# One run of products per group, dt in four column tiles, and two scalings moved to VectorE in a Mamba-2 and attention trunk

## The chip, the cores and the metric

The kernel runs on one core of a Trainium2 chip. The metric is the device time of one execution in microseconds (us). Five engines take part: TensorE (PE in the profile, its weight loads PEld), VectorE (DVE), ScalarE (ACT), GpSimd (POOL) and SyncE (SP, which only issues DMAs here). Each engine works through its own list of instructions in order and waits on semaphores for the others.

## The reference

Two layers on a 512 x 1024 input: a Mamba-2 mixer with a chunked state-space scan, then differential attention, then a final norm. The change lies in the first layer, of which this is the core (cut):

```python
h = rms_norm(x, norm_g)
zxbcdt = h @ w_in                                   # z, xBC, and dt_raw (32 heads)
xbc = silu(causal_depthwise_conv(xbc, conv_w, conv_b))
dt = softplus(dt_raw + dt_bias)
a = -exp(a_log)
# per chunk:
acs = cumsum(a * dt);  decay = exp(where(causal, acs_l - acs_s, -inf))
y_diag = (C_l . B_s) * decay  @  (x * dt)           # products inside the chunk
y_off  = C_l . state * exp(acs)
y = y_diag + y_off + d_skip * x
y = group_rms_norm(y * silu(z)) * gate_norm_g       # 8 groups of 4 heads
x = x + y @ w_out
```

## The kernel before

All of the first layer is kept on the chip. Sequence positions are cut into four chunks of 128 (`NQ`), the 32 heads into eight groups of four (`G`, `R`). Large products are split in a high and a low float32r part and run as three matmuls of 128x128 by 512 (`mm3`); small products of the scan are plain float32, which the profile shows as two records each.

TensorE's dense stream in the first layer is `z0 g0 g1 z1 g2 g3 z2 g4 o0 g5 z3 g6 g7 o1 o2 o3`: `z` are gate projections (tile `pz`), `g` the B, C and x projections of one group (tile `pg`), `o` the output projections (tile `po`). Each needs four banks of PSUM from a pool of four (`mm_bank`). A `pg` bank comes free when VectorE has run the convolution on it: one multiplication (`pg<-pg,ar_row`), a pass on ScalarE, and three `xc` steps with 511, 510 and 509 columns, of which the last frees the bank. Weights arrive by DMA in tile `raw`; ScalarE makes the high part `whi`, VectorE the low part `wlo`.

Beside the stream runs `ssd(g)`, the scan of a group. `pcb` is C.B; `pxt` turns x, and VectorE makes `xdt` (x times dt) and `dx` (x times the skip factor) from it; GpSimd makes `xe` for the states; `psA` and `psB` are the chunk states, `pyd` the products inside the chunks (64 columns of weights each, so two lie side by side in the array), `po1` and `po2` (both shown as `po<-hst,xc`) the parts from earlier chunks. Then `dx` is summed, gated with `zs`, its squares summed on ScalarE (`tmp,ss<-dx`), `rsqrt` makes the factor in a chain of small VectorE instructions (`v`, `y_i`, `y_y`, `y_c`, last `y_y`), ScalarE scales the four chunks (`tmp<-dx,y_y`), `pyt` turns them, and `yh`, `yl` are the high and low part for the output projection.

`dt` is made once, near the start, and all groups need it. Its chain is: product `ps_dt`, tile `pre` (times `ar_row`, the 1/rms of each position along a row, which comes from the product `aps_r`), a softplus on ScalarE (`e`) and VectorE (`q`, `pl`, `dtp`), a running sum `acs`, a DMA to memory and back spread over the partitions (`dec`), GpSimd's subtraction and mask on `dec`, ScalarE's exponential of `dec`.

A scheduler sets the order on every engine by its own timing model; `T.on`, `V.on` and `A.on` tell it to keep the marked instructions of that engine in the order in which they are written. Before the change no instruction of the scan is marked. In the second layer nearly everything is. `with tc.high_priority()` prefers the last group.

```python
class Ordered:                                       # line 45
    ...
            if self.on:
                self.tc.keep_in_program_order(i)
order_a = "z0 g0 g1 z1 g2 g3 z2 g4 o0 g5 z3 g6 g7 o1 o2 o3".split()
def mm_bank(name):
    return psum.tile([P, 512], F32, tag="mm", name=name, bufs=4)
def long_bank(name):
    return psum.tile([P, 512], F32, tag="long", name=name)
```

`ss_bank` gives a bank from a pool of three for the small products; `long_bank` is a single bank. Almost all instructions pass through `Ordered`, so the profile puts them on its line 55; they are told apart by their tiles.

Of the kernel before, what the change touches and what calls it, by code (L numbers as in the profile page):

```python
# [9 lines left out]
F32 = mybir.dt.float32  # L10
F32R = mybir.dt.float32r
I32 = mybir.dt.int32
AF = mybir.ActivationFunctionType
ALU = mybir.AluOpType
# [3 lines left out]
P = 128  # L18
# [3 lines left out]
KD = D // P  # L22
G = 8
R = 4
HD = 64
H = 32
NQ = 4
# [11 lines left out]
C_GA, C_GK, C_GB, C_GG, C_SG, C_DTB, C_AL, C_CB, C_CW = 0, 8, 16, 24, 40, 41, 42, 43, 75  # L39
# [24 lines left out]
def trunk(ctx, tc, x, x_t, par, w_dt, w_in, w_out, w_kvqg, w_bo, d_skip, lam_qk, fin_g, out):  # L64
    nc = tc.nc
    V, A, T = (Ordered(tc, e) for e in (nc.vector, nc.scalar, nc.tensor))
# [14 lines left out]
    def ss_bank(name):  # L81
        turns[0] += 1
        tag = "mm" if turns[0] % turns[1] >= 3 else "ss"
        return psum.tile([P, 512], F32, tag=tag, name=name, bufs=3 if tag == "ss" else 4)

    def long_bank(name):
        return psum.tile([P, 512], F32, tag="long", name=name)
# [10 lines left out]
    prm = const.tile([P, C_CB], F32, name="prm")  # L98
# [142 lines left out]
    def rsqrt(v, n, tag, bufs=2):  # L241


        y = small.tile([P, n], F32, tag=f"{tag}_y", name=f"{tag}_y", bufs=bufs)
        c = small.tile([P, n], F32, tag=f"{tag}_c", name=f"{tag}_c", bufs=bufs)
        iy = small.tile([P, n], I32, tag=f"{tag}_i", name=f"{tag}_i", bufs=bufs)

        def vyy():
            if n == 1:
                V.scalar_tensor_tensor(out=c, in0=y, scalar=v, in1=y, op0=ALU.mult, op1=ALU.mult)  # L250
            else:
                V.tensor_tensor(out=c, in0=y, in1=v, op=ALU.mult)
                V.tensor_tensor(out=c, in0=c, in1=y, op=ALU.mult)

        V.tensor_scalar(out=iy, in0=v.bitcast(I32), scalar1=1, scalar2=None, op0=ALU.logical_shift_right)
        V.tensor_scalar(out=y.bitcast(I32), in0=iy, scalar1=-1.0, scalar2=float(0x5F3759DF - 2 ** 31), op0=ALU.mult, op1=ALU.add)
        vyy()
        V.scalar_tensor_tensor(out=c, in0=c, scalar=-10.0 / 3.0, in1=c, op0=ALU.add, op1=ALU.mult)
        V.scalar_tensor_tensor(out=y, in0=c, scalar=5.0, in1=y, op0=ALU.add, op1=ALU.mult)
        vyy()  # L260
        V.scalar_tensor_tensor(out=y, in0=c, scalar=-64.0 / 3.0, in1=y, op0=ALU.add, op1=ALU.mult)
        return y
# [39 lines left out]
    def scales(tag, ss):  # L302

        V.tensor_scalar(out=ss, in0=ss, scalar1=ROOT2 / D, scalar2=ROOT2 * EPS, op0=ALU.mult, op1=ALU.add)
        col = res.tile([P, NT], F32, tag="r_col", name=f"{tag}r_col")
        V.tensor_copy(col, rsqrt(ss, NT, "y"))
        w = small.tile([P, NT + 1, P], F32, tag="wide", name=f"{tag}diag", bufs=2)
        GP.memset(w[:, NT], 1.0)
        for t in range(NT):
            GP.tensor_tensor(out=w[:, t], in0=ident, in1=col[:, t:t + 1].to_broadcast([P, P]), op=ALU.mult)  # L310
        ps = long_bank(f"{tag}ps_r")
        T.matmul(ps, lhsT=w[:, NT], rhs=w[:, 0:NT].rearrange("p t n -> p (t n)"), start=True, stop=True)
        row = res.tile([P, S], F32, tag="r_row", name=f"{tag}r_row")
        A.copy(row, ps)
        return col, row
# [14 lines left out]
    def new_h(tag):  # L330
        return [res.tile([P, KD, S], F32R, tag=f"hT_{i}", name=f"{tag}_{i}") for i in ("hi", "lo")]
# [9 lines left out]
    hh, hl = new_h("a")  # L341
# [4 lines left out]
    bp2 = bctx.enter_context(tc.tile_pool(name="bp2", bufs=2))  # L346
# [17 lines left out]
    xt = [bp2.tile([P, 2, S], F32, tag="yl", name=f"xt{i}", bufs=4) for i in range(4)]  # L364
# [27 lines left out]
    for t in range(NT):  # L392
        squares(ss, t)
    r_col, r_row = scales("a", ss)
    V.tensor_scalar(out=sg1, in0=prm[:, C_SG:C_SG + 1], scalar1=0.5 * (1.0 - LAM0), scalar2=None, op0=ALU.mult)
    dtw_raw = sm.tile([P, KD, H], F32, name="dtw_raw")
# [1 line left out]

    dw = bp2.tile([P, KD, 2, 2, H], F32R, tag="yh", name="dw", bufs=4)
    for k in range(KD):
        src = dtw_raw[:, k, :].unsqueeze(1).to_broadcast([P, 2, H])
        gk = prm[:, C_GA + k:C_GA + k + 1]
        A.activation(dw[:, k, :, 0], src, AF.Copy, scale=gk)
        V.scalar_tensor_tensor(out=dw[:, k, :, 1], in0=src, scalar=gk, in1=dw[:, k, :, 0].bitcast(F32), op0=ALU.mult, op1=ALU.subtract)
    ps_dt = ss_bank("ps_dt")
    for k in range(KD):
        w = dw[:, k].rearrange("p a b h -> p (a b h)")
        T.matmul(ps_dt, lhsT=w, rhs=hh[:, k, :], start=k == 0, stop=False)  # L410
        T.matmul(ps_dt, lhsT=w, rhs=hl[:, k, :], start=False, stop=k == KD - 1)

    pre = sm.tile([P, P], F32, name="pre")
    for c in range(NQ):
        sl, hi, lo = (slice(i * H, (i + 1) * H) for i in (c, 0, 1))
        cs = slice(c * P, (c + 1) * P)
        A.copy(pre[sl, :], ps_dt[lo, cs])
        V.tensor_tensor(out=pre[sl, :], in0=ps_dt[hi, cs], in1=pre[sl, :], op=ALU.add)
    for c in range(NQ):
        sl = slice(c * H, (c + 1) * H)  # L420
        V.tensor_tensor(out=pre[sl, :], in0=pre[sl, :], in1=r_row[sl, c * P:(c + 1) * P], op=ALU.mult)
    V.tensor_scalar(out=pre, in0=pre, scalar1=prm[:, C_DTB:C_DTB + 1], scalar2=None, op0=ALU.add)
    e1 = sm.tile([P, P], F32, name="e1")
    A.activation(e1, pre, AF.Abs)
# [136 lines left out]
    def ssd(g):  # L561
        bc, cc, x0, x1 = conv_out.pop(g)
        xc = (x0, x1)
        dec, een, _ = decs.pop(g)
# [3 lines left out]
        for c in range(NQ):  # L568
            cs = slice(c * P, (c + 1) * P)
# [8 lines left out]
        for j in range(2):  # L578
            pxt = ss_bank(f"pxt{g}_{j}")
            for c in range(NQ):  # L580
# [5 lines left out]
                            in1=dsk[:, h2].unsqueeze(1).unsqueeze(3).to_broadcast([P, NQ, 2, HD]), op=ALU.mult)  # L586
# [6 lines left out]
        hst = bp.tile([P, 3, R, HD], F32, tag="hst", name=f"hst{g}")  # L593
        hsf = hst.rearrange("p c h e -> p c (h e)")
        psA = ss_bank(f"psA{g}")
        for c in range(2):
            T.matmul(psA[:, c * 256:(c + 1) * 256], lhsT=bt[:, c, :], rhs=xe[:, c].rearrange("p h e -> p (h e)"), start=True, stop=True)
        A.copy(hsf[:, 0], psA[:, 0:256])
# [6 lines left out]

        ss4 = small.tile([P, NQ], F32, tag="ss4", name=f"ss4{g}")
        tmp = bp.tile([P, NQ, R, HD], F32, tag="tmp", name=f"tmp{g}")
        pyd = []
        for q in range(2):
            pyd.append(ss_bank(f"pyd{g}_{q}"))  # L610
            for c in (2 * q, 2 * q + 1):
                for h in range(R):
                    o = (c % 2) * 256 + h * HD

                    for r in (slice(0, 64), slice(64, 128)):
                        T.matmul(pyd[q][r, o:o + HD], lhsT=dec[:, h, c, r], rhs=xdt[:, c, h, :], start=True, stop=True)
            dq = dx[:, 2 * q:2 * q + 2].rearrange("p c h e -> p c (h e)")
            V.tensor_tensor(out=dq, in0=pyd[q].rearrange("p (c e) -> p c e", c=2), in1=dq, op=ALU.add)
        if g % 2 and g < G - 1:
# [5 lines left out]
        for c in (2, 3):  # L625
            T.matmul(po2[:, (c - 2) * 256:(c - 1) * 256], lhsT=cc[:, c * P:(c + 1) * P], rhs=hsf[:, c - 1], start=True, stop=True)
        V.tensor_tensor(out=tmp[:, 1], in0=po1[:, 256:512].rearrange("p (h e) -> p h e", e=HD),
                        in1=eacs_tok[:, 1, hs].unsqueeze(2).to_broadcast([P, R, HD]), op=ALU.mult)
        V.tensor_tensor(out=tmp[:, 2:4], in0=po2.rearrange("p (c h e) -> p c h e", h=R, e=HD),
                        in1=eacs_tok[:, 2:4, hs].unsqueeze(3).to_broadcast([P, 2, R, HD]), op=ALU.mult)  # L630
        u = dx.rearrange("p c h e -> p c (h e)")
        tm = tmp.rearrange("p c h e -> p c (h e)")
# [6 lines left out]
        V.tensor_scalar(out=v4, in0=ss4, scalar1=ROOT2 / 256.0, scalar2=ROOT2 * EPS, op0=ALU.mult, op1=ALU.add)  # L639
        r4 = rsqrt(v4, NQ, "y")  # L640
        for c in range(NQ):
            A.activation(tm[:, c], u[:, c], AF.Copy, scale=r4[:, c:c + 1])
        yh = bp2.tile([P, 2, S], F32R, tag="yh", name=f"yh{g}", bufs=4)
        yl = bp2.tile([P, 2, S], F32R, tag="yl", name=f"yl{g}", bufs=4)
        for j in range(2):
# [9 lines left out]
    for g in range(G):  # L655
        until(f"g{g}")
        if g < G - 1:
            ssd(g)
        else:
            with tc.high_priority():  # L660
                ssd(g)
# [3 lines left out]
    hh, hl = new_h("b")  # L665
# [273 lines left out]
    def half(t, n):  # L939
        hs = slice(n * 512, (n + 1) * 512)  # L940
        return x_tok[:, t, hs], fg[:, hs], ot[t][:, hs], out[t * P:(t + 1) * P, hs]
# [59 lines left out]
    h = DH - 1  # L1001
# [59 lines left out]
    y, f, o, dst = half(3, 0)  # L1061
# [71 lines left out]
```

## Time and profile before

| | |
|---|---|
| median of 3 runs | 729.46 us (729.12 to 731.79) |
| profiled execution | 729.15 us, span 727.0 us |
| granted TensorE clock | 0.998 |
| PE busy | 713.5 us, 98% of the span |
| DVE, ACT, POOL busy | 528.0 (73%), 433.7 (60%), 117.7 (16%) us |
| first layer | to about 430 us |
| second layer | from about 430 us |

In the rows of the timeline the columns are: start in us from the start of the span, length in us of the row (several like instructions are merged, with their count), engine, line, operation, out<-in, shapes, count, and in brackets the idle time of the engine before it with what ended it. A PE row is longer than the distance to the next row, because matmuls overlap in the pipeline; the rate of the engine is the distance between starts. A float32 matmul has two records, so sixteen of them stand as x32.

### The profile page before, as it was taken

Reading aid. Unit: us, or ns where it says so; the run is one execution under the profiler, and the core shown is the slowest. Engines: PE = TensorE matmul, PEld = TensorE weight load, DVE = VectorE, ACT = ScalarE, POOL = GpSimd, SP = SyncE. Lnnn points to the kernel's source line nnn. Section 1 sums busy time; section 2 is a strip of 40 time slices with the busy share of each in tenths; the row PEclk is TensorE's granted clock in tenths of the full one; section 3 lists DMA queues with packets and bytes.
Section 4 is the critical chain, followed back from the end, with each engine's and each line's share of the span. In section 5 each row is a group of like instructions: output and inputs, shape, how many; then the busy total and the mean of one; then the engine's idle time right before and its main releaser. Section 6 shows DMA issues by size and latency. Waiting matters only on the chain.

```text
span 727.0 us, 10819 instructions
## 1 busy us (share of the span) xinstructions
PE 713.5 (98%) x3989; PEld 593.1 (82%) x3989; DVE 528.0 (73%) x1202; ACT 433.7 (60%) x965; POOL 117.7 (16%) x158
## 2 busy tenths in 40 slices
PE   9999999999999999999999999999999999999996
PEld 7787888888888888887788869888988898889874
DVE  4688964979479668569995846657667857785886
ACT  5948573654735527527534348667766756756566
POOL 0108241412315024150110101000000000000002
PEclk9999999999999999999999999999999999999999
DMA  8634313314133231231122310331221131122003
GB/s 302 233 131 162 116 59 117 117 58 175 58 117 116 95 137 60 91 142 59 59 70 105 116 59 9 117 115 59 94 82 58 59 117 59 59 90 85 29 1 115
DMA packets 12916, 70.86 MB, mean 97 GB/s; under 512 B 1728, under 2 KB 2496, under 8 KB 5312
## 3 DMA queue, kind: packets, MB, share of 16 engines
q1 hardware_dynamic: 12576, 69.90, 26.5%
q8 instruction: 31, 0.51, 0.3%
q10 hardware_dynamic: 288, 0.28, 0.1%
q14 instruction: 21, 0.17, 0.1%
HBM read 68.02 MB, written 2.16 MB: 97 GB/s over the span
## 4 chain that ended last, share of the span: by engine, by line
PE 90%; DVE 7%; ACT 1%; issue 1%; POOL 0%; ACTq 0%; DVEq 0%; POOLq 0%
PE pg L55 21%; PE po L55 14%; PE pz L55 12%; PE pt L55 7%; PE pv L55 6%; PE pq L55 6%; PE pk L55 6%; PE pb L55 3%; PE sc L55 3%; PE pyd L55 2%; PE pc L55 2%; DVE wlo L55 2%; DVE xc L55 2%; PE pyt L55 1%; PE pxt L55 1%; PE psA L55 1%
## 5 line engine op out<-in xcount | busy, mean ns | idle before, releaser
L55 DVE SCALAR_TENSOR_TENSOR wlo<-raw,prm,whi 128x512 fp32r<-128x512 f32 (+1 forms) x256 | 150.4, 633 | 52.7 <-ACT whi L55 51.3
L55 ACT ACTIVATE whi<-raw,prm 128x512 fp32r<-128x512 f32 (+1 forms) x256 | 136.8, 606 | 81.4 <-PE pg L55 30.1
L55 PE MATMUL pg<-a_hi,whi 128*128 128x512 f32 x256 | 103.3, 404 | 1.5 <-DVE y_c L55 1.5
L55 PE MATMUL pg<-a_hi,wlo 128*128 128x512 f32 x256 | 102.3, 402 | 0.0
L55 PE MATMUL pg<-a_lo,whi 128*128 128x512 f32 x256 | 102.3, 400 | 0.0
L55 DVE SCALAR_TENSOR_TENSOR xc<-pg,prc,xc 128x511 f32<-128x511 f32 (+2 forms) x96 | 69.6, 738 | 4.8 <-ACT xc L55 4.4
L55 PEld LDWEIGHTS pg<-a_hi,whi 128*128 128x128 f32 x256 | 48.1, 188 | 13.1 <-issue 1.9
L55 PEld LDWEIGHTS pg<-a_hi,wlo 128*128 128x128 f32 x256 | 48.1, 188 | 11.0
L55 PEld LDWEIGHTS pg<-a_lo,whi 128*128 128x128 f32 x256 | 48.1, 188 | 10.7
L55 PE MATMUL po<-whi,yh 128*128 128x512 f32 x128 | 51.4, 402 | 1.5 <-DVE xc L55 0.8
L55 PE MATMUL po<-wlo,yh 128*128 128x512 f32 x128 | 51.1, 399 | 0.0
L55 PE MATMUL po<-whi,yl 128*128 128x512 f32 x128 | 50.4, 398 | 0.0
L55 PE MATMUL pz<-wlo,a_hi 128*128 128x512 f32 x128 | 50.3, 399 | 0.0
L55 PE MATMUL pz<-whi,a_lo 128*128 128x512 f32 x128 | 49.8, 398 | 0.0
L55 PE MATMUL pz<-whi,a_hi 128*128 128x512 f32 x128 | 49.6, 401 | 0.0
L971 POOL TENSOR_TENSOR ot<-ot,fg 128x512 f32<-128x512 f32 x4 | 5.1, 1289 | 256.9 <-ACT ot L55 256.9
L55 ACT ACTIVATE s<-s,mx 128x128 f32<-128x128 f32 (+3 forms) x64 | 35.5, 556 | 9.6 <-DVE mx L55 9.1
L55 ACT ACTIVATE xc<-pg,prc 128x512 f32<-128x512 f32 x32 | 24.6, 773 | 26.6 <-DVE pg L55 26.5
L589 POOL TENSOR_TENSOR xe<-xdt,tok 128x256 f32<-128x256 f32 x24 | 17.3, 749 | 139.6 <-DVE xdt L55 139.6
L55 DVE CUSTOM_DVE_ANT_0 s<-sc,bias 128x128 f32<-128x128 f32 (+3 forms) x64 | 29.4, 488 | 12.2 <-PE sc L55 11.7
L55 ACT ACTIVATE xc<-xc 128x512 f32<-128x512 f32 x32 | 20.0, 629 | 28.3 <-DVE xc L55 28.2
L55 PE MATMUL pv<-whi,b_hi 128*128 128x256 f32 x128 | 36.6, 286 | 0.0
(243 smaller groups left out, 1719.7 us busy)
## 6 DMA issues: line engine op xcount, KB each, us to landing
raw<-in_w_in SPq DMA_DIRECT2D x23, 1024.0 KB, 4.8
raw<-in_w_kvqg SPq DMA_DIRECT2D x16, 1024.0 KB, 4.8
dec<-acs_d SPq DMA_DIRECT2D x8, 1024.0 KB, 4.8
raw<-in_w_out SPq DMA_DIRECT2D x8, 1024.0 KB, 4.8
raw<-in_w_bo SPq DMA_DIRECT2D x4, 1024.0 KB, 4.8
x_tok<-in_x SPq DMA_DIRECT2D x4, 512.0 KB, 9.3
out<-ot SPq DMA_DIRECT2D x7, 256.0 KB, 2.4
raw<-in_w_in SPq DMA_DIRECT2D x4, 256.0 KB, 5.8
```

The costliest lines, as they stand in the source:

```text
L55: i = op(*args, **kw)
L589: GP.tensor_tensor(out=xe[:, c], in0=xdt[:, c], in1=toe_tok[:, c, hs].unsqueeze(2).to_broadcast([P, R, HD]), op=ALU.mult)
L971: GP.tensor_tensor(out=o, in0=o, in1=f, op=ALU.mult)
```

## The change

There are three edits.

1. **dt.** The weights are multiplied with the norm's gain by one VectorE instruction, in place of sixteen on ScalarE and VectorE that made a high and a low part. The product is plain float32 from the untouched input `xt`: for each of eight slices of 128 rows, four matmuls of 32 columns of weights, one for each 128 positions, which write to four groups of 32 partitions. So `pre` needs no sum of two parts and no copy: VectorE multiplies the product with `ar_row` straight from PSUM. The products are marked to stay behind `aps_r`.
2. **Products inside the chunks.** Both halves of `pyd` come behind one another, the second half first, with no other matmul between (all are marked, with `psA` and `psB` ahead of them). One half lies in `long_bank` now.
3. **Last group.** Chunks 1 and 3 are scaled by VectorE and no longer by ScalarE.

```diff
         ps = long_bank(f"{tag}ps_r")
+        T.on = True
         T.matmul(ps, lhsT=w[:, NT], rhs=w[:, 0:NT].rearrange("p t n -> p (t n)"), start=True, stop=True)
+        T.on = False
...
-    dw = bp2.tile([P, KD, 2, 2, H], F32R, tag="yh", name="dw", bufs=4)
+    V.tensor_tensor(out=dtw_raw, in0=dtw_raw, in1=prm[:, C_GA:C_GA + KD].unsqueeze(2).to_broadcast([P, KD, H]), op=ALU.mult)
+    ps_dt = ss_bank("ps_dt")
+    T.on = True
     for k in range(KD):
-        src = dtw_raw[:, k, :].unsqueeze(1).to_broadcast([P, 2, H])
-        gk = prm[:, C_GA + k:C_GA + k + 1]
-        A.activation(dw[:, k, :, 0], src, AF.Copy, scale=gk)
-        V.scalar_tensor_tensor(out=dw[:, k, :, 1], in0=src, scalar=gk, in1=dw[:, k, :, 0].bitcast(F32), op0=ALU.mult, op1=ALU.subtract)
-    ps_dt = ss_bank("ps_dt")
-    for k in range(KD):
-        w = dw[:, k].rearrange("p a b h -> p (a b h)")
-        T.matmul(ps_dt, lhsT=w, rhs=hh[:, k, :], start=k == 0, stop=False)
-        T.matmul(ps_dt, lhsT=w, rhs=hl[:, k, :], start=False, stop=k == KD - 1)
+        for c in range(NQ):
+            T.matmul(ps_dt[c * H:(c + 1) * H, 0:P], lhsT=dtw_raw[:, k, :], rhs=xt[k // 2][:, k % 2, c * P:(c + 1) * P],
+                     start=k == 0, stop=k == KD - 1)
+    T.on = False
     pre = sm.tile([P, P], F32, name="pre")
     for c in range(NQ):
-        sl, hi, lo = (slice(i * H, (i + 1) * H) for i in (c, 0, 1))
-        cs = slice(c * P, (c + 1) * P)
-        A.copy(pre[sl, :], ps_dt[lo, cs])
-        V.tensor_tensor(out=pre[sl, :], in0=ps_dt[hi, cs], in1=pre[sl, :], op=ALU.add)
-    for c in range(NQ):
         sl = slice(c * H, (c + 1) * H)
-        V.tensor_tensor(out=pre[sl, :], in0=pre[sl, :], in1=r_row[sl, c * P:(c + 1) * P], op=ALU.mult)
+        V.tensor_tensor(out=pre[sl, :], in0=ps_dt[sl, 0:P], in1=r_row[sl, c * P:(c + 1) * P], op=ALU.mult)
...
         psA = ss_bank(f"psA{g}")
+        T.on = True
...
-        pyd = []
-        for q in range(2):
-            pyd.append(ss_bank(f"pyd{g}_{q}"))
+        pyd = [ss_bank(f"pyd{g}_0"), long_bank(f"pyd{g}_1")]
+        for q in (1, 0):
             for c in (2 * q, 2 * q + 1):
-                for h in range(R):
+                for h in reversed(range(R)):
                     o = (c % 2) * 256 + h * HD
                     for r in (slice(0, 64), slice(64, 128)):
                         T.matmul(pyd[q][r, o:o + HD], lhsT=dec[:, h, c, r], rhs=xdt[:, c, h, :], start=True, stop=True)
+        T.on = False
+        for q in range(2):
...
         for c in range(NQ):
-            A.activation(tm[:, c], u[:, c], AF.Copy, scale=r4[:, c:c + 1])
+            if g == G - 1 and c % 2:
+                V.tensor_scalar(out=tm[:, c], in0=u[:, c], scalar1=r4[:, c:c + 1], scalar2=None, op0=ALU.mult)
+            else:
+                A.activation(tm[:, c], u[:, c], AF.Copy, scale=r4[:, c:c + 1])
```

The scheduler lays all of the first layer anew for this; the order in the second layer is the same on every engine. Three places show how.

Near the start, ScalarE before: `zs` are the gates of the first projection, `whi` the next weights, `e` begins the softplus of dt.

```order
L55 ACTIVATE zs_2_1_426<-pz_2_139,ar_col 128x256
L55 COPY pre<-ps_dt 32x128 x2
L55 COPY ar_row<-aps_r 128x512
L55 COPY pre<-ps_dt 32x128 x2
L55 ACTIVATE whi_370<-raw_368,prm 128x512 x4
L55 ACTIVATE zs_3_0_440<-pz_3_140,ar_col 128x256
L55 ACTIVATE zs_3_1_442<-pz_3_140,ar_col 128x256
L55 ACTIVATE e_316<-pre 128x128
```

ScalarE now, the same place:

```order
L55 ACTIVATE zs_2_1_418<-pz_2_139,ar_col 128x256
L55 ACTIVATE whi_362<-raw_360,prm 128x512 x4
L55 ACTIVATE zs_3_0_432<-pz_3_140,ar_col 128x256
L55 ACTIVATE zs_3_1_434<-pz_3_140,ar_col 128x256
L55 COPY ar_row<-aps_r 128x512
L55 ACTIVATE e_308<-pre 128x128
```

The four copies of `pre` are gone, and the copy of `ar_row` has moved behind the four `whi` and the two `zs`.

The sixth group's end and the convolution beside it, VectorE before: `xc_2984` works on the bank `pg_0_2896`, and its step with 509 columns frees it; `v`, `y_i`, `y_y` and `y_c` are the small instructions of the sixth group's factor.

```order
L55 TENSOR_TENSOR pg_0_2896<-pg_0_2896,ar_row 128x512
L55 TENSOR_SCALAR v_2741<-ss_2645 128x4
L55 TENSOR_SCALAR y_i<-v_2741 128x4
L55 TENSOR_SCALAR y_y<-y_i 128x4
L55 TENSOR_TENSOR y_c<-y_y,v_2741 128x4
L55 TENSOR_TENSOR y_c<-y_c,y_y 128x4
L55 TENSOR_TENSOR pg_1_2897<-pg_1_2897,ar_row 128x512
L55 SCALAR_TENSOR_TENSOR xc_2984<-pg_0_2896,prc,xc_2984 128x511
L55 SCALAR_TENSOR_TENSOR y_c<-y_c 128x4
L55 SCALAR_TENSOR_TENSOR xc_2984<-pg_0_2896,prc,xc_2984 128x510
...
L55 SCALAR_TENSOR_TENSOR xc_2984<-pg_0_2896,prc,xc_2984 128x509
```

VectorE now (`xc_2976` on `pg_0_2888` is the same convolution):

```order
L55 TENSOR_TENSOR pg_0_2888<-pg_0_2888,ar_row 128x512
L55 TENSOR_TENSOR tmp_2638<-po_2717,tok 128x512
L55 SCALAR_TENSOR_TENSOR xc_2976<-pg_0_2888,prc,xc_2976 128x511
L55 SCALAR_TENSOR_TENSOR xc_2976<-pg_0_2888,prc,xc_2976 128x510
L55 TENSOR_TENSOR pg_1_2889<-pg_1_2889,ar_row 128x512
L55 SCALAR_TENSOR_TENSOR xc_2976<-pg_0_2888,prc,xc_2976 128x509
...
L55 TENSOR_SCALAR v_2733<-ss_2637 128x4
```

The bank is freed ahead of the small instructions now, which now begin thirteen rows after the step that frees it.

The last group on TensorE before, from the second state product; `po_1_0`, `po_1_1` and `po_1_2` belong to the stream's `o2`:

```order
L55 MATMUL psB_3394<-xe_3379,bt_3361 128x256
L55 MATMUL pyd_0_3400<-xdt_3363,dec_2702 64x64 x16
L55 MATMUL po_1_0_3688<-whi_3542,yl_2760 128x512
...
L55 MATMUL po_1_2_3716<-wlo_3543,yh_2292 128x512
L55 MATMUL pyd_1_3418<-xdt_3363,dec_2702 64x64 x16
L55 MATMUL po_3436<-hst_3387,xc_3291 128x256
L55 MATMUL po_3438<-hst_3387,xc_3291 128x256 x2
```

TensorE now:

```order
L55 MATMUL psB_3386<-xe_3371,bt_3353 128x256
L55 MATMUL pyd_1_3393<-xdt_3355,dec_2694 64x64 x16
L55 MATMUL pyd_0_3392<-xdt_3355,dec_2694 64x64 x16
L55 MATMUL po_3428<-hst_3379,xc_3283 128x256
L55 MATMUL po_1_1_3694<-wlo_3535,yh_2284 128x512
```

The two halves of `pyd` are one run, where fifteen matmuls of the stream lay between them; it is so in all eight groups.

## The prediction

> **What bounds the kernel now.** I read the page's busy times, then its chain of work that ended last, then the waits of TensorE in the first 430 us, and last the timeline around each wait.
>
> ```profile
> PE 713.5 (98%) x3989; PEld 593.1 (82%) x3989; DVE 528.0 (73%) x1202; ACT 433.7 (60%) x965; POOL 117.7 (16%) x158
> PE 90%; DVE 7%; ACT 1%; issue 1%; POOL 0%; ACTq 0%; DVEq 0%; POOLq 0%
> ...
> PE pg L55 <- DVE y_c L55: 1.5, 1, 1.5
> PE po L55 <- DVE xc L55: 0.8, 1, 0.8
> PE pyt L55 <- ACT tmp L55: 0.7, 1, 0.7
> PE pxt L55 <- ACT xc L55: 0.6, 1, 0.6
> ```
>
> TensorE is the bound: busy 98%, and 90% of the chain. A change can gain only where TensorE issues less or waits less. The last four rows (total us, count, longest) are its longest waits in the first layer, under 4 us in all. The second layer keeps its order on every engine, so I count nothing there.
>
> **1. The two halves of the products come together.**
>
> ```profile
> 79.33 0.50 PE L55 MATMUL pg<-a_hi,whi 128*128 128x512 f32 x1
> 79.66 0.40 PE L55 MATMUL pg<-a_lo,whi 128*128 128x512 f32 x1
> 79.89 0.40 PE L55 MATMUL pg<-a_hi,wlo 128*128 128x512 f32 x1
> ...
> 84.09 0.40 PE L55 MATMUL pg<-a_hi,wlo 128*128 128x512 f32 x1
> 84.42 1.15 PE L55 MATMUL pyd<-xdt,dec 128*64 128x64 f32 x32
> 85.50 1.56 PE L55 MATMUL po<-hst,xc 128*128 128x256 f32 x6
> ...
> L55 PE MATMUL pyd<-xdt,dec x512: 222/222/270, 78.2 to 408.4; 128*64 128x64 f32 x171
> ```
>
> A matmul of 512 columns is followed by the next after 0.23 us (79.66 to 79.89). The same matmul ahead of the 64-column products takes 0.33 (84.09 to 84.42): 0.10 to enter that form. Thirty-two records start within 1.15 - 0.22 = 0.93 us, yet the next matmul starts after 1.08 (85.50): 0.15 to leave less the 0.03 of a record, 0.12. The matmul after that exit then takes 0.33 instead of 0.23 (79.33 to 79.66): another 0.10. One visit costs 0.32 us. There are 16 visits (512 records by 32), and 8 remain: -8 x 0.32 = -2.6 us. Bounds: 0.35 a visit gives -2.8; if the exit alone were saved, -1.8.
>
> **2. dt.** It removes 16 matmuls of 512 columns, 16 x 0.233 = 3.7 us, and adds 32 products of 128 columns. No row shows a tile of 32 columns; the nearest is the 64-column pair, 0.93 / 16 = 0.058 us a product of 64 columns. At 128 columns and the same overlap of two: 32 x 0.116 = 3.7 us. Four overlapping: 1.9. None: 7.5. With 0.3 for the visit, TensorE gives from -1.5 to +4.1. I take four, since they lie in four different column groups as the pair lies in two: about -1.3 with some waiting for `aps_r`. But this does not reach the end, because of what stands behind dt:
>
> ```profile
> 26.84 0.39 PE L55 MATMUL ps_dt<-a_hi,dw 128*128 128x512 f32 x1
> 31.04 1.02 PE L55 MATMUL aps_r<-adiag 128*128 128x512 f32 x2
> 32.82 0.59 ACT L55 COPY ar_row<-aps_r 128x512 f32<-128x512 f32 x1
> 34.66 2.56 ACT L55 ACTIVATE whi<-raw,prm 128x512 fp32r<-128x512 f32 x4
> 37.26 0.84 ACT L55 ACTIVATE zs<-pz,ar_col 128x256 f32<-128x256 f32 x2
> 39.95 0.23 DVE L55 TENSOR_SCALAR q<-e 128x128 f32<-128x128 f32 x1 [1.68 <-ACT e L55]
> 54.88 0.19 POOL L551 COPY dec<-dec 128x8 f32<-128x8 f32 x1 [24.95 <-DMA dec<-acs_d]
> 60.09 0.46 ACT L55 COPY bt<-pbt 128x384 f32<-128x384 f32 x1
> 63.64 1.92 ACT L55 ACTIVATE dec<-dec 128x2056 f32<-128x2056 f32 x1 [1.79 <-POOL dec L554]
> 66.87 1.15 ACT L55 ACTIVATE xc<-xc 128x512 f32<-128x512 f32 x2
> 67.55 0.66 PE L55 MATMUL pxt<-ident,xc 128*128 128x128 f32 x4 [0.61 <-ACT xc L55]
> ```
>
> The chain runs through all of them: softplus, running sum, memory and back, GpSimd (idle 24.95 us until the data came), ScalarE's exponential (idle 1.79), then the `xc` that stands behind it on ScalarE, then `pxt`, where TensorE waits. What TensorE saves before 67.55 becomes a longer wait there unless the chain shortens too. Now `ps_dt` ends near 32 instead of before 31, but ScalarE has no use for it sooner: it does the four `whi` (2.56), two `zs` (0.84) and the copy of `ar_row` (0.59) first, all behind the first gates, which puts `q` at about 39.5 for 39.95, 0.4 sooner. The `bt` copy (0.46) now stands between the exponential of `dec` and `xc`, and gives the 0.4 back. So 0 for dt. Bounds: -1.3 if the chain kept up with TensorE; +1.5 if the tiles do not overlap, when `ps_dt` ends near 38, about 1.5 later than the `ar_row` copy wants it. The sixteen weight splittings and the four copies that fall away on ScalarE and VectorE lie beside the dense stream before `pxt`; I count nothing for them.
>
> The bare TensorE rows would put this at -1.3 and the sum at 724.7; the chain puts it at 0. On this the Trainium skill, "TensorEngine Tiling (Array Packing)", section PSUM Bottleneck, says that tiles speed TensorE up but not what empties PSUM, which may then be the limit. The trace agrees as far as it can: ScalarE's rows above, not TensorE's, set the time of `q`.
>
> **3. The sixth group's wait.**
>
> ```profile
> 323.89 0.97 DVE L55 TENSOR_SCALAR y_i<-v 128x4 int32<-128x4 int32 x1
> 326.49 0.55 DVE L55 TENSOR_TENSOR y_c<-y_c,y_y 128x4 f32<-128x4 f32 x1
> 329.07 1.40 DVE L55 SCALAR_TENSOR_TENSOR xc<-pg,prc,xc 128x511 f32<-128x511 f32 x2
> ...
> 328.69 0.40 PE L55 MATMUL pg<-a_hi,wlo 128*128 128x512 f32 x1
> 330.62 0.47 PE L55 MATMUL pg<-a_hi,whi 128*128 128x512 f32 x1 [1.53 <-DVE y_c L55]
> ```
>
> The small instructions of four columns ran ahead of the convolution that frees the bank, for up to 0.97 us each. They now follow it. From 328.69 to 330.62 is 1.93, less 0.23 is 1.7 lost; I take 1.5 back. Bounds: 0 if VectorE is late at that place anyway, -1.7.
>
> **4. The bank of the first output projection.**
>
> ```profile
> 354.38 4.01 DVE L55 SCALAR_TENSOR_TENSOR xc<-pg,prc,xc 128x511 f32<-128x511 f32 x6
> ...
> 361.20 0.40 PE L55 MATMUL po<-whi,yl 128*128 128x512 f32 x1
> 362.43 0.47 PE L55 MATMUL po<-whi,yh 128*128 128x512 f32 x1 [0.83 <-DVE xc L55]
> ```
>
> Here 1.23 - 0.23 = 1.0 us is lost: `po` needs a bank that an `xc` step frees. In the new order fourteen steps of VectorE stand between the seventh group's second `xdt` and the step that frees the third bank (three `dx`, four `xc`, four `wlo` and others; 4.01 / 6 = 0.67 us for the long ones, about 9.3 in all), and `xdt` itself is done some 2.2 us after `pxt`: 11.5 us. TensorE has from `pxt` to that bank 27 matmuls (6.3), the state products (1.5) and the joined run (2.0): 9.8. The wait becomes about 1.7 to 2.0, on the next bank: +1.0. Bounds: -1.0 (no wait) to +2.0.
>
> **5. Less filling ahead of the state products.** Groups three and seven had 31 and 33 dense matmuls between `pxt` and `psA`; now 17 and 16, 16 x 0.233 = 3.7 us. `psA`, `psB` and the whole run are held in order behind GpSimd's `xe`.
>
> ```profile
> 347.19 0.69 DVE L55 TENSOR_TENSOR xdt<-pxt,tok 128x512 f32<-128x512 f32 x1 [1.70 <-PE pxt L55]
> 350.49 2.22 POOL L589 TENSOR_TENSOR xe<-xdt,tok 128x256 f32<-128x256 f32 x3 [22.28 <-DVE xdt L55]
> 355.84 1.02 PE L55 MATMUL psA<-xe,bt 128*128 128x256 f32 x4
> ```
>
> Before, `xe` was done at 352.7, 3.1 us ahead of `psA`; that cover goes. In the new order six convolution steps stand ahead of the first `xdt`, of which the last four follow the third `pg` bank by 2.6 us: `xdt` starts some 0.9 us after `pxt`, the second ends at 3.5, `xe`'s three parts at 4.3, 5.1 and 5.9. TensorE asks for them at about 4.5, 4.9 and 5.4: 0.5 us lost in the seventh group, almost none in the third. I take +0.5. Bounds: 0, and +2 x 1 if VectorE is 1 us late at both; more is the slower rival.
>
> **6. The last group's end.**
>
> ```profile
> 420.40 0.40 PE L55 MATMUL po<-whi,yl 128*128 128x512 f32 x1
> 420.96 1.71 ACT L55 ACTIVATE tmp<-dx,y_y 128x256 f32<-128x256 f32 x4 [1.81 <-DVE y_y L55]
> 421.52 1.63 PE L55 MATMUL pyt<-ident,tmp 128*128 128x128 f32 x8 [0.72 <-ACT tmp L55]
> 423.73 0.51 PE L55 MATMUL po<-whi,yh 128*128 128x512 f32 x1 [0.57 <-ACT yh L55]
> ```
>
> ScalarE scales four chunks at 0.43 each, and `pyt` follows chunk by chunk. VectorE takes two of them beside it: 2 x 0.43 = 0.86 sooner, -0.9. Bounds: -0.3 (VectorE's two end no earlier than ScalarE's third would) to -2.2 (all that is lost here beside the transposes: 3.33 from 420.40 to 423.73, less 0.23 and less eight transposes at about 0.11).
>
> **Sum.** -2.6 + 0 - 1.5 + 1.0 + 0.5 - 0.9 = -3.5 us. The profiled execution took 729.15, so 725.65; the median of the runs lies 0.3 above it: 726.0.
>
> **The rivals.**
>
> *The gain is handed on.* The sixth group's wait stays (+1.5) and VectorE is about half a us late at the two places of step 5 (+1): 728.5. For it: VectorE works through convolutions with hardly a gap there. Against: the 1.70 us that it idled ahead of `xdt`.
>
> *Everything shows.* No wait for the output projection's bank (-2.0 against my sum) and the whole of the last group's loss above the transposes (-1.3): 722.7. For it: VectorE and ScalarE are both relieved near the start. Against: step 4's count of steps.
>
> *The 32-column tiles do not overlap*: +1.5, 727.5. For it: nothing in the rows shows a width of 32. The Trainium skill, the same page, Gotcha 2, says that column tiling excludes the fast weight load; no row here separates that. Against: the 64-column pair at 0.058 us, with loads of its own.
>
> *Slower.* VectorE comes to `xdt` about 4 us late in groups three and seven. TensorE then stands at `psA` with the run and all dense work behind it, 2 x 4 = 8: 734. My gain is gone at 1.75 us of lag in each, and it is slower by 0.5% from 3.6 on. For it: the filling lost is just 3.7, and six convolution steps moved ahead of `xdt`. Against: again the 1.70 us of idleness, and that those steps wait for TensorE themselves.
>
> **How the numbers follow.** Forecast, 724.6 to 727.2: 0.46. Handed on: 0.24. Everything shows: 0.13. No overlap: 0.05. Slower: 0.12. A measurement of this kernel tells about 0.5%, 3.65 us, from no change: the bounds are 725.8 and 733.1. Not quite half of the forecast's share lies below 725.8 with all of the "everything shows": faster 0.35; slower 0.12, with 0.01 for a long lag in the handed-on case 0.13; within 0.52. The range from 722.6 to 730.0 leaves out the slower case and the tails, 0.2.
>
> **What would show it.** One row of 64 `pyd` records per group, entered and left once; `ps_dt` behind `aps_r` in about 2 us for its 64 records; `pxt` near 67.5 with a longer wait, about 2; no wait near 327 for a `pg` bank; a wait near 358 for `po` of about 2; `psA` of the seventh group up to 0.5 late; the chunks of `tmp` on two engines and 1.3 us from last to next `po` beyond the transposes. A wait of over 2 us at `psA`, or `ps_dt` of over 4 us, would make the forecast wrong.

## The result: 719.9 us, 1.4% faster

The changed kernel takes 719.9 us (median of 4 runs, 719.73 to 720.57); the kernel before, beside it, 730.0 (729.12 to 731.79). The ratio is 0.986, interval 0.9839 to 0.9881. The prediction was 726.0 with a range from 722.6 to 730.0: the direction was right, the size was less than half of what was measured, and the time lies below the range.

The two profiled executions have spans of 727.0 and 718.2 us, 8.8 apart. The other 1 us or so of the medians is in the kernel before: in 70 runs of it in the later comparisons it took 728 to 734 us, with medians between 730.5 and 731.1, while the changed kernel stayed between 719.7 and 720.8. The profiled execution that the prediction was built on (729.15) was one of the better ones of its kernel; the second profile of the same kernel, E4 below, shows where a longer one loses its time. One execution, of E7, took 784.71 us at a granted clock of 0.85 and is left out of its ratio.

### The profile page after: what moved, and what is told of

Same layout as the page of the kernel before. It is cut to its first block, busy times and chain, and to the rows that moved or that the text cites. A ratio compares the mean times of both kernels' runs of the same rounds, so it can differ in the third digit from the quotient of the medians.

```text
span 718.2 us, 10908 instructions
## 1 busy us (share of the span) xinstructions
PE 708.0 (99%) x4037; PEld 591.2 (82%) x4037; DVE 521.2 (73%) x1193; ACT 429.4 (60%) x951; POOL 112.9 (16%) x158
## 4 chain that ended last, share of the span: by engine, by line
PE 88%; ACT 5%; DVE 4%; DMA 2%; issue 1%; SPq 0%; ACTq 0%; DVEq 0%
PE pg L55 21%; PE po L55 16%; PE pz L55 9%; PE pt L55 7%; PE pq L55 6%; PE pv L55 6%; PE pk L55 6%; PE pb L55 3%; PE sc L55 3%; PE pyd L55 2%; PE pc L55 2%; ACT whi L55 1%; DMA raw<-in_w_in 1%; PE pxt L55 1%; PE pyt L55 1%; PE psA L55 1%
## 5 line engine op out<-in xcount | busy, mean ns | idle before, releaser
L583 POOL TENSOR_TENSOR xe<-xdt,tok 128x256 f32<-128x256 f32 x24 | 14.1, 613 | 162.0 <-DVE xdt L55 162.0
L547 POOL TENSOR_TENSOR dec<-dec,tok 128x512 f32<-128x512 f32 x32 | 36.0, 1154 | 0.6
```

Of the source, the lines that this page charges most:

```text
L547: GP.tensor_tensor(out=dec[:, h], in0=dec[:, h], in1=acs_tok[:, :, R * g + h].unsqueeze(2).to_broadcast([P, NQ, P]), op=ALU.subtract)
L583: GP.tensor_tensor(out=xe[:, c], in0=xdt[:, c], in1=toe_tok[:, c, hs].unsqueeze(2).to_broadcast([P, R, HD]), op=ALU.mult)
```

## The profile after

First the page's busy times and its chain, then TensorE's waits in the first 430 us (total us, count, longest), its warming left out:

```profile
PE 708.0 (99%) x4037; PEld 591.2 (82%) x4037; DVE 521.2 (73%) x1193; ACT 429.4 (60%) x951; POOL 112.9 (16%) x158
...
PE 88%; ACT 5%; DVE 4%; DMA 2%; issue 1%; SPq 0%; ACTq 0%; DVEq 0%
```

```profile
PE pz L55 <- ACT whi L55: 0.5, 1, 0.5
PE po L55 <- ACT yh L55: 0.5, 1, 0.5
```

All four waits that the prediction quoted are gone: `pg` for `y_c`, `po` for `xc`, `pyt` for `tmp`, `pxt` for `xc`. What is left is 0.5 at the start and 0.5 at the end. I compared the same dense matmul (1536 of them, in nearly the same order) in both traces and took the shift at places between the groups:

| term | predicted | read from the two traces |
|---|---|---|
| start, up to 24 us | 0 | +0.3 |
| dt: TensorE | 0, with the next row | -1.6 |
| dt: wait of the first `pxt` | | -0.5 |
| eight visits less | -2.6 | -2.8 |
| sixth group's wait | -1.5 | -1.8 |
| wait of the first output projection | +1.0 | -1.1 |
| filling ahead of `psA` | +0.5 | 0 |
| last group's end | -0.9 | -1.4 |
| sum | -3.5 | -8.9 |

dt and the run of products in the timeline of TensorE; the run is that of the seventh group:

```profile
29.44 1.02 PE L55 MATMUL aps_r<-adiag 128*128 128x512 f32 x2
30.40 1.96 PE L55 MATMUL ps_dt<-xt,dtw_raw 128*32 128x128 f32 x64
65.71 0.66 PE L55 MATMUL pxt<-ident,xc 128*128 128x128 f32 x4
...
354.06 0.59 PE L55 MATMUL psB<-xe,bt 128*128 128x256 f32 x2
354.58 2.08 PE L55 MATMUL pyd<-xdt,dec 128*64 128x64 f32 x64
356.60 0.50 PE L55 MATMUL po<-whi,yh 128*128 128x512 f32 x1
356.93 0.39 PE L55 MATMUL po<-wlo,yh 128*128 128x512 f32 x1
```

The 64 records of dt take 1.96 us, so four groups of columns do overlap (1.9 was the price for four, 3.7 for two). The two halves of `pyd` have one entry and one exit. `pxt` starts 1.84 us sooner than before and has no bracket: nothing was waited for.

## The experiments

### Each edit alone

E1 makes edit 1 alone (the first part of the diff), E2 edit 2 alone, E3 edit 3 alone, E5 edits 2 and 3.

> Edit 1 alone (dt in four column tiles behind aps_r); the order of everything behind the first group stays as before. Theory A, from the trace of after: TensorE gains about 1.4 us near the start (16 x 0.233 = 3.7 us out, 1.96 us in, 0.3 for the visit) and keeps it, because the chain of dt was late in the profile of before through one slow store of the running sum (3.4 us to land, where the other three took 1.4 to 1.5) and not through the work on ScalarE: -1.4 to -2.2 us, pxt of the first group starts near 66 with no wait. Theory B, the prediction's: the chain sets the time of pxt, TensorE's gain turns into a wait there: 0 +- 0.5 us, pxt at 67.3 to 67.6 with about 2 us of wait.

> Edit 2 alone (one run of products per group). Theory A: it carries most of the gain, since the new order of VectorE comes with it: 8 visits less (-2.7), the sixth group's wait gone (-1.7), the wait for the output projection's second bank gone (-1.0): -5.4 us, and nothing before 70 us changes. Theory B, the prediction's terms: -2.6 for the visits, -1.5 for the sixth group, +1.0 for the bank, +0.5 ahead of psA: -2.6 us in all, with a wait of about 2 us near 360.

> Edit 3 alone (two of the last group's four scalings on VectorE). Theory A: the four scalings take 1.0 us instead of 1.8 from the factor to the last tmp, TensorE gains 0.8 us between the last po ahead of pyt and the first po behind it. The remaining 0.6 us of what after gains there come with the order of edit 2 (the factor is ready earlier). Theory B: all 1.4 us come from the scaling: -1.4 us.

> After without edit 1: edits 2 and 3 only; against the kernel before with 730. Theory A (the dt edit is worth about 1.4 us on TensorE and about 1.3 us through a chain that ends sooner, so that pxt of the first group does not wait): 722.8 of edit 2 alone, less 0.8 for the scaling: 722.0, that is 2.1 us above after; pxt of the first group waits 1.0 to 1.8 us. Theory B (edit 1 alone measured 0, so it is worth nothing): 719.9, as after.

| | median us | beside it, before | ratio, interval |
|---|---|---|---|
| E1, dt | 730.75 | 730.98 | 0.9992, 0.9975 to 1.0009 |
| E2, run of products | 722.81 | 730.98 | 0.9884, 0.9862 to 0.9906 |
| E3, scaling | 728.51 | 730.98 | 0.9969, 0.9953 to 0.9986 |
| E5, edits 2 and 3 | 721.56 | 731.1 | 0.987, 0.9847 to 0.9892 |

Edit 2 carries most of it. In its trace every group is 0.33 to 0.36 us shorter, the sixth group's wait, the output projection's and that of `pyt` are gone, and one of 1.2 us at the first `pxt` is left. Theory A was right on the places. Its 5.4 us were reckoned from one profile; the spans of the two profiles differ by 6.0 (727.0 and 721.0), and the medians by 8.2, because the kernel before takes 730.98 in the median, 1.8 above its profiled execution.

E3 gains 0.66 at its place: from the last `po` ahead of `pyt` to the next are 2.67 us, where 3.33 were. So theory A was right in kind (0.8), and theory B's 1.4 is out. The medians differ by more, 2.5 us with an interval from 1.0 to 3.4, than that place shows; where the rest comes from is open.

In E5 the time came near theory A's (721.56 for 722.0), and theory B's 719.9 is out: beside edits 2 and 3, edit 1 is worth about 1.6 us. But the wait at the first `pxt` that theory A asked for is not in the profile. That execution is the fastest of the four (720.58; the others took 721.5 to 721.85, and have no profile).

E1 measured nothing, and looks like theory B; but its trace is not the one that B described. `pxt` starts at 65.82 and TensorE is 1.75 us ahead from there to 195 us, as theory A had it. Then it loses 0.9 at the third group's `pyt`, and 2.0 at a place where the profile of before shows no wait: it stands for 1.85 us at 233.59 for a `po` bank, which `x_tok` on VectorE frees. The rows of GpSimd and VectorE ahead of it, before and then in E1:

```profile
227.65 4.47 POOL L553 TENSOR_TENSOR dec<-dec,tok 128x512 f32<-128x512 f32 x4
226.77 1.40 DVE L55 SCALAR_TENSOR_TENSOR wlo<-raw,prm,whi 128x512 fp32r<-128x512 f32 x2
```

```profile
224.78 5.22 POOL L547 TENSOR_TENSOR dec<-dec,tok 128x512 f32<-128x512 f32 x4
224.91 1.54 DVE L55 SCALAR_TENSOR_TENSOR wlo<-raw,prm,whi 128x512 fp32r<-128x512 f32 x1
226.37 1.27 DVE L55 TENSOR_TENSOR dx<-dx,zs 128x256 f32<-128x256 f32 x1
227.56 2.99 DVE L55 SCALAR_TENSOR_TENSOR wlo<-raw,prm,whi 128x512 fp32r<-128x512 f32 x2
```

The order is the same on VectorE. In E1 GpSimd's subtraction came 2.9 us sooner and lay beside `wlo`, which took 1.5 us each instead of 0.7; GpSimd itself took 5.22 for 4.47.

But this collision is not edit 1's. E13 (below) is the kernel before up to this place, without edit 1, and has it too:

```profile
225.04 5.21 POOL L554 TENSOR_TENSOR dec<-dec,tok 128x512 f32<-128x512 f32 x4
227.82 2.99 DVE L55 SCALAR_TENSOR_TENSOR wlo<-raw,prm,whi 128x512 fp32r<-128x512 f32 x2
233.85 0.51 PE L55 MATMUL po<-whi,yh 128*128 128x512 f32 x1 [1.85 <-DVE x_tok L55]
```

In the orders without edit 1 the subtraction began at 227.65 (before), 227.09 (E4), 226.09 (E3) and 225.04 (E13), and TensorE waited 0, 0.2, 1.1 and 1.8 us. It begins when the load of `dec` has landed, and that load took 6.5 us in the profile of before, 5.2 in E4, 5.1 in E3, and 4.7 in E13 and in E1. The profile of before happened to be free of the wait.

### GpSimd beside VectorE

E9 and E10 take that subtraction away, in the kernel before and in E1; all other instructions keep their order.

```diff
             for h in range(R):
-                GP.tensor_tensor(out=dec[:, h], ... op=ALU.subtract)
+                if g != 5:
+                    GP.tensor_tensor(out=dec[:, h], ... op=ALU.subtract)
```

> The kernel before, without GpSimd's subtraction on dec for the sixth group (four instructions near 227 us; the products of that group come out wrong by that). Every other instruction stands in the same order on all engines. Theory A (while GpSimd subtracts, VectorE's instructions on SBUF take about twice as long, and where this meets the wlo and dx steps near 227 TensorE waits at 233 for po): wlo there stays at 0.74 us each, no wait at 233; since that wait was 0, 0.4 and 1.2 us in three profiles of this order, the median falls by 0.3 to 1.0 us. Theory B (GpSimd does not matter there): nothing changes.

> Edit 1 alone, again without GpSimd's subtraction on dec for the sixth group. Theory A: edit 1 gained 1.7 us up to 205 us and lost it at 233, where TensorE waited 2.0 us because GpSimd started 2.7 us earlier beside VectorE's wlo; without the subtraction the wait goes, and the time is 1.4 to 1.8 us below that of before without the same subtraction. Theory B (the loss has another cause): no difference to before without the subtraction, a wait near 233 stays.

E9: 730.27 us beside 730.79 (0.9998, 0.9983 to 1.0013). E10: 729.06 (0.998, 0.9962 to 0.9998). In E10 the wait at 233 is 0.2 instead of 1.9 us, and edit 1 is worth 1.2 us between the medians of the two, a little under the 1.4 to 1.8 of theory A; with twelve runs of each that spread over 3.8 us, about 0.9 either way is uncertain. So it is shown that edit 1 gains 1 to 2 us on TensorE up to 195 us, and that the collision makes the wait at 233. That E1's median gains nothing because of this wait is not shown, since the kernel before often has it as well; why it gains nothing stays open. E9's own expectation of 0.3 to 1.0 is not confirmed: 0.5 lies inside the uncertainty.

E7 and E13 look at the sixth group's wait. E7 joins the run in the sixth group alone (`if g == 5` around edit 2). E13 cuts the subtraction for the eighth group, which runs at that time, to 2 of 128 columns.

> The kernel before, with the joined run in the sixth group alone (one visit of sixteen less). The order around it changes: the step that frees the pg bank stands ahead of most of the small instructions of the sixth group's factor, but the seventh group keeps 33 dense matmuls ahead of psA. Theory A (what edit 2 gains beyond the visits is VectorE's order at that place): the wait near 330 goes, -0.3 for the visit and -1.7 for the wait: about -2.0 us, while the wait of 1.0 near 362 stays. Theory B (the gain is the visits'): -0.3 us.

> The kernel before, with GpSimd's subtraction on dec of the eighth group, which runs near 321 to 326 us, cut to 2 of 128 columns (the products of that group come out wrong by that). Up to the sixth group's small instructions VectorE's order is the same as before; behind them one convolution step changes places, by which the bank comes free 0.66 us sooner, and from there on the order is another, so only the place near 330 is read. Theory A (the subtraction holds VectorE's instructions on SBUF: v, y_i, y_y, y_c took 0.4 to 1.0 us each and wlo 0.95): the small ones take 0.15 to 0.2 us each, the wait of 1.5 us near 330 is gone. Theory B (order alone): the small ones stay at 0.4 to 1.0 us, the wait falls by 0.66 to about 0.9 us.

E7 measured 732.04 beside 731.1 (1.0011, 0.9996 to 1.0026): theory A fell. The bank's step stood ahead of most of the small instructions, and the wait came back in three pieces of 1.0, 1.8 and 0.7 us; some 1.5 us more went to a stretch at half clock behind them, of which E4 below has another. The rows of E7:

```profile
317.57 5.42 POOL L553 TENSOR_TENSOR dec<-dec,tok 128x512 f32<-128x512 f32 x4
317.77 5.77 DVE L55 SCALAR_TENSOR_TENSOR wlo<-raw,prm,whi 128x512 fp32r<-128x512 f32 x4 [1.29 <-ACT whi L55]
```

Four `wlo` took 1.44 each beside the subtraction, and the whole convolution came late behind them. In the changed kernel the same subtraction meets other work:

```profile
316.99 4.08 POOL L547 TENSOR_TENSOR dec<-dec,tok 128x512 f32<-128x512 f32 x4
318.21 1.53 DVE L55 SCALAR_TENSOR_TENSOR xc<-pg,prc,xc 128x511 f32<-128x511 f32 x2 [0.26 <-ACT xc L55]
...
329.96 2.06 DVE L55 SCALAR_TENSOR_TENSOR wlo<-raw,prm,whi 128x512 fp32r<-128x512 f32 x3
334.15 0.16 DVE L55 TENSOR_SCALAR y_i<-v 128x4 int32<-128x4 int32 x1
```

The `xc` steps, which read PSUM, take their usual time beside it, and `wlo` (0.69) and the small instructions (0.16; 0.97 before) come when GpSimd is through. The Trainium skill, "SBUF — State Buffer", section Who interferes with whom, says that a VectorE instruction with two inputs in SBUF contends with a GpSimd instruction that reads SBUF, and one with at most one such input, outside the two-port modes, does not. The trace agrees for the long ones: `wlo` and `dx<-dx,zs` have two, `xc<-pg,prc,xc` one. Of the small ones it leaves a question: in before, `y_i<-v` and `y_y<-y_i` have one input, and took 0.97 and 0.98 beside the subtraction all the same.

```profile
320.94 4.92 POOL L553 TENSOR_TENSOR dec<-dec,tok 128x512 f32<-128x512 f32 x4
324.90 0.98 DVE L55 TENSOR_SCALAR y_y<-y_i 128x4 int32<-128x4 int32 x1
```

Whether they ran in such a two-port mode no run here shows.

In E13 (727.83 us) the wait near 330 is gone, and the five small instructions from `v` take 1.96 us in place of 3.45: 0.55 each for three of them, beside GpSimd's mask, and not the 0.2 that theory A asked for. But TensorE came to that place 0.8 us later against VectorE than before (a wait of 1.8 at 233 lay ahead of it), and the step that changed places gives 0.66; those two could also have taken away most of the 1.7. So that the subtraction slows these instructions is shown; that it alone made the wait is not.

### The store of the running sum

In the profile of before, the load of `dec` that follows the store of the running sum `acs_d` was issued at 50.65, in that of after at 48.63. The issues of SyncE, before and after:

```profile
45.89 1.75 SPq L450 DMA_DIRECT2D acs_d<-acs  x4
50.65 0.81 SPq L549 DMA_DIRECT2D dec<-acs_d  x2
```

```profile
45.65 1.81 SPq L444 DMA_DIRECT2D acs_d<-acs  x4
48.63 0.81 SPq L543 DMA_DIRECT2D dec<-acs_d  x2
```

The last of the four stores landed 3.36 us after its issue before, 1.58 after. The packets show what stood in its way: a 16 KB load of instructions (queue q8; the store is on q1), from 48.31 to 49.54. The last two data packets of the store start at 49.53 and 49.58, all others by 48.35. By their number these loads are TensorE's: from before to after its matmuls and weight loads on the page go from 7978 to 8074 and the loads from 31 to 32, some 250 to each. No other engine has a fifth of that number, and none has more of it than before. Edit 1 gives TensorE 48 more records with their weight loads by that time, and the load comes at 40.12.

E4 runs the kernel before again, E11 leaves out four of eight steps of the polynomial (`for m in (7, 5, 3)` in place of seven values), so that the store comes sooner, and E8 adds twelve one-column products to TensorE's warming, to move the load.

> The kernel before once more, unchanged, for a second profile. Theory A (the fourth store of the running sum was slow by chance in that one execution): here it lands 1.4 to 1.6 us after its issue, the load of dec starts near 48.9 instead of 50.65, and pxt of the first group waits less than 0.2 us instead of 0.6. Theory B (the store is slow because of what runs beside it in this order): it again takes about 3.4 us and pxt waits about 0.6 us.

> Edit 2 alone, with four of the eight steps of the softplus's polynomial left out (dt is a little off by that), so that the running sum and its four stores come about 1.3 us sooner, while TensorE's load of instructions stays near 48 us; some rows of the first 70 us are laid otherwise. Only the store is compared. Theory A (a store is slow when the 16 KB load of instructions starts before its packets are through): the stores are issued at 44.4 to 46.2, their packets are through by 47.6, the last lands 1.4 to 1.7 us after its issue. Theory B: 3.1 to 3.5 us as in edit 2 alone.

> Edit 2 alone, with twelve more products of one column among TensorE's warming products at the very start, 24 records more. They move the point at which TensorE's instructions are loaded by DMA (16 KB at a time, 256 instructions) some 5 to 6 us ahead of the stream. The start is laid a little differently by this, so the time as a whole is not compared, only the store of the running sum. Theory A (the load of instructions, 1.25 us on one DMA queue, stands ahead of packets of the store when both fall together): it comes near 43 to 44 us, the last of the four stores lands 1.4 to 1.7 us after its issue and not 3.1 to 3.5, and pxt of the first group waits at least 1 us less than the 1.2 of edit 2 alone. Theory B (the store is slow for another reason): it lands after 3.1 to 3.5 us again.

| | load of instructions | store issued | last store lands after | first `pxt` waits |
|---|---|---|---|---|
| before | 48.31 | 47.21 | 3.36 | 0.6 |
| E4 | 47.71 | 47.41 | 3.25 | 1.8 |
| E2 | 48.03 | 47.37 | 3.10 | 1.2 |
| E3 | 47.65 | 46.52 | 3.48 | 1.2 |
| E5 | 48.03 | 46.61 | 1.50 | 0 |
| E11 | 47.59 | 45.59 | 1.50 | 0 |
| E1 | 40.48 | 47.07 | 1.50 | 0.5 |
| after | 40.12 | 46.97 | 1.58 | 0 |

E4 decides for theory B, with a longer wait than B's: the store is slow again, and the wait 1.8, not 0.6. E11 decides for the load of instructions: the stores are through before it begins, the last lands in 1.50, and the kernel takes 721.0 us in that execution, 1.8 below E2. In E5 the store escaped narrowly: there the load began 1.4 us behind the last store's issue, in the slow ones 0.3 to 1.1. E8 missed: its load stayed at 47.65 because the whole start moved by 4.4 us. All four stores took about 3.5 us there, beside a 1 MB load of weights, issued at 43.07, whose packets ran until 47.2; it tells nothing of this.

E4 also shows where a longer execution of the kernel before loses its time. Its span is 2.9 us above that of the first profile (729.9 for 727.0). TensorE starts 0.7 ahead there, then loses 1.1 at the first `pxt`, 0.5 at 233 and 1.9 near 330. There the wait is 0.4 longer, and then dense matmuls start 0.43 us apart instead of 0.23:

```profile
331.89 0.62 PE L55 MATMUL pg<-a_hi,whi 128*128 128x512 f32 x1 [1.89 <-DVE y_c L55]
332.31 0.63 PE L55 MATMUL pg<-a_lo,whi 128*128 128x512 f32 x1
332.74 0.63 PE L55 MATMUL pg<-a_hi,wlo 128*128 128x512 f32 x1
```

From 332.05 the granted clock is 0.5, for 3.41 us, which costs about 1.5 us. The profiles of E7 and E10 have such a stretch near there too (335.83, 330.66); of all others only E8 has one between 15 us and 700 us, at 75.54, behind its wait of 2.4 us for the first `pxt`. Of the 70 runs of the kernel before, the 23 with a mean granted clock of 0.996 or less took 731.6 us in the median, the other 47 took 730.5. So a part of what edit 2 gains in the medians may be that these stretches go with the wait near 330; this was not tested.

### The order of dt's products

E6 swaps the two loops of edit 1, so that eight products of one column group follow one another.

```diff
-    for k in range(KD):
-        for c in range(NQ):
+    for c in range(NQ):
+        for k in range(KD):
             T.matmul(ps_dt[c * H:(c + 1) * H, 0:P], ...
```

> After, with the 32 products of dt in another order: all eight of one group of 32 columns, then the next group. Nothing else differs. Theory A (four groups of columns overlap, and only because neighbouring products lie in different groups): the 64 records take about 7.5 us instead of 1.96, TensorE comes to pxt 5.5 us later, and the running sum is late by some 2: 719.9 + 5.5 = 725.4 us. Theory B (a product of 32 columns is short by itself, whatever stands beside it): still 1.96 us, 719.9.

It took 723.8 us (0.9903, 0.9885 to 0.9921), 3.9 above after, and the row of dt is

```profile
30.35 5.95 PE L55 MATMUL ps_dt<-xt,dtw_raw 128*32 128x128 f32 x64
```

4.0 us longer than in the changed kernel, all of it in the result. Theory A is right in kind: the overlap shrinks when neighbours lie in the same group. Its 7.5 us, doubled twice from the 64-column pair, was too much. The Trainium skill, "TensorEngine Tiling (Array Packing)", section Key Properties, says that different tiles work in parallel; the two rows agree, 5.95 over 1.96 is 3.0.

### After, without edit 3, and after again

> After without edit 3. Theory A: edit 3 saves what the four scalings take less, seen at the last group's end as 0.65 us between edit 2 alone and edits 2 and 3: 720.0 + 0.65 = 720.65 us. Theory B, the prediction's 0.86 us for two scalings of 0.43: 720.9. Theory C (the y chain, not the scaling, sets the end, as for the whole 1.4 us that after gained there): 720.0.

> The changed kernel once more, unchanged, beside the kernels of this call: 719.9, no wait of the first group's pxt, no wait of over 0.7 us in the first layer. If the absence of waits was chance, one of 1 us or more shows here, and the median is 721 or more.

E12: 720.0 us (0.9864, 0.9844 to 0.9884). The first `pxt` waits 0.6 in its trace, no other wait is over 0.5. E14: 720.98 us, 1.0 above it, from another comparison. The place at the end shows 0.66 us between their traces, and the rest of E14's lies ahead of 110 us, where the edit changes nothing. So theory A's size holds by place; by the medians alone B's 0.86 could not be told from it. Theory C is out. The end of the last group, before a `po` and behind `pyt`, in after:

```profile
412.50 0.16 DVE L55 SCALAR_TENSOR_TENSOR y_y<-y_c,y_y 128x4 f32<-128x4 f32 x1
412.70 0.62 DVE L55 TENSOR_SCALAR tmp<-dx,y_y 128x256 f32<-128x256 f32 x2
412.76 0.91 ACT L55 ACTIVATE tmp<-dx,y_y 128x256 f32<-128x256 f32 x2 [1.61 <-DVE y_y L55]
412.93 0.40 PE L55 MATMUL po<-whi,yl 128*128 128x512 f32 x1
414.87 0.50 PE L55 MATMUL po<-whi,yh 128*128 128x512 f32 x1 [0.46 <-ACT yh L55]
```

From 412.93 to 414.87 are 1.94 us, where 3.33 were. The last step of the factor starts 0.43 ahead of TensorE's last `po` (0.30 behind it before), and the scalings take 0.97 instead of 1.71. No version that was tried beats after.

## Why the prediction was wrong, point by point

**1, the visits: right.** 2.8 for 2.6; a visit costs 0.35.

**2, dt: wrong by 2.1 us.** The TensorE part was right (four groups overlap, -1.3 predicted, -1.6 found). The step that failed is "So 0 for dt." That the chain sets the time of `pxt` was right: TensorE still waits for it in E1 (0.5) and in E12 (0.6). `q` moved less than worked out (39.71 for 39.95; I had 39.5), and `bt` did stand behind the exponential. But I took the way from the running sum to GpSimd's data as it stood in one profile. It held 1.8 us of a store behind a load of instructions, and the edit moves that load by changing TensorE's count; the load of `dec` was issued 2.0 us sooner and `pxt` came 1.84 sooner. I had the row with GpSimd's 24.95 us of idleness and never asked what the DMA in its bracket had waited for.

**3, the sixth group: right in size** (1.8 for 1.5), wrong in its reason, at least in part: E7 has the order that I gave as the reason and still waits there, while the small instructions alone take 1.5 us less in E13 when most of the subtraction is left out. Which part of the 1.8 is order and which is GpSimd stays open.

**4, the output projection's bank: wrong by 2.1 us, and in sign.** Fourteen steps do stand where I counted them. The mistake is which bank TensorE needs there:

```profile
350.39 0.39 PE L55 MATMUL po<-whi,yh 128*128 128x512 f32 x1
354.47 0.74 DVE L55 SCALAR_TENSOR_TENSOR xc<-pg,prc,xc 128x509 f32<-128x509 f32 x1
356.60 0.50 PE L55 MATMUL po<-whi,yh 128*128 128x512 f32 x1
357.46 0.67 DVE L55 TENSOR_TENSOR x_tok<-po,x_tok 128x512 f32<-128x512 f32 x1
359.48 0.40 PE L55 MATMUL po<-whi,yh 128*128 128x512 f32 x1
```

The first `po` tile runs from 350.39, ahead of the joined run. The second can have the bank that the `xc` step at 354.47 frees, 1.4 us before it is asked for. The third, at 359.48, does not want the third convolution's bank, which comes free at about 361.6 and would have been late: the first `po` tile is already added to `x_tok` at 358.1, and its bank is free. I had assumed banks in fixed turn. Which tile has which bank is read from these times; the profile does not name the banks.

**5, the filling: +0.5 predicted, 0 found.** The times were right: `pxt` at 348.59, `xdt` 0.92 behind it (0.9 worked out), `psA` at 353.19, 4.6 behind (4.5):

```profile
348.59 1.03 PE L55 MATMUL pxt<-ident,xc 128*128 128x128 f32 x8
349.51 0.68 DVE L55 TENSOR_TENSOR xdt<-pxt,tok 128x512 f32<-128x512 f32 x1
352.12 1.76 POOL L583 TENSOR_TENSOR xe<-xdt,tok 128x256 f32<-128x256 f32 x3 [27.12 <-DVE xdt L55]
353.19 1.03 PE L55 MATMUL psA<-xe,bt 128*128 128x256 f32 x4
```

Only `xe` was quicker, 1.76 us for three where the row of before had 2.22, which was all the margin. The slower rival hung on VectorE's lag at this place; there was none.

**6, the end: -1.4 for -0.9.** E14 and E3 give the scaling 0.66 each; the other 0.73 is there in E2 with edit 2 alone (2.60 us for 3.33), where the factor came sooner with the new order. I had taken that as unchanged.

**The sum** left out what several terms share: in E2 the order that edit 2 brings takes the losses of steps 3, 4 and half of 6 away at once, and my range treated the good ends as separate strokes of luck. It also started from one profile, which E4 shows to be a good one. The rival "everything shows" named the bank and the end, at 722.7 and 0.13, and still had dt at 0.

## What to carry to other kernels

A wait on a DMA is a row to be followed to the packets: a small store of 1.5 us took 3.0 to 3.5 when a load of an engine's instructions ran among its packets, and an edit that changes an engine's count of instructions can move such loads (edit 1 moved one by 8 us). Where GpSimd and VectorE both work on SBUF, ask what the order lays beside GpSimd: here `wlo` took twice as long there, and the `xc` steps, which read PSUM, did not. An edit that measures 0 alone may have gained and lost: read the shift at places along the trace before calling it worthless, and look whether profiles without the edit have the same loss. A kernel whose runs spread over 6 us is not priced from one profile.

## What the runs showed of the hardware that I had not expected

- A 16 KB load of instructions, by its count TensorE's, takes 0.9 to 1.5 us near the store, up to 1.9 elsewhere. In six profiles (before, E2, E3, E4, E7, E9) it began 0.3 to 1.1 us behind the issue of the last of four 16 KB stores, and that one landed in 3.0 to 3.5 us; in nine others it lay elsewhere, and that store landed in 1.5 to 1.6.
- Plain float32 products of 32 columns of weights: 64 records in 1.96 us when neighbours lie in four column groups, in 5.95 when they follow one another in the same group.
- `wlo` took 1.44 to 1.54 us beside GpSimd's subtraction, 0.69 to 0.74 without it, and the subtraction 1.3 us for 1.0; VectorE's `xc` steps, which read PSUM, kept their time.
- In E4, E7 and E10 the granted clock of TensorE fell to 0.5 for 3.41 us, 0.2 to 1.4 us behind the end of waits near 330 (1.9 in E4 and E10; 1.0, 1.8 and 0.7 in E7); behind the wait of 1.5 there in before it did not, nor behind that of 1.9 at 233 in E1.
